# A decoder step on one core: layer 0's single-bank feed-forward stretch begins at part 1 instead of part 2

## Chip, cores and metric

One core of one Trainium2 chip. The metric is the device time of the whole program in microseconds. The kernel computes one inference step of a two-layer decoder for a prompt of 1024 tokens and eight sample tokens; nearly all of its work is matrix products on TensorE (PE).

## Reference

Layer 0 has a gated recurrence and attention to 256 memory tokens, layer 1 stick-breaking attention over a shared key and value store and again the memory attention. Behind each mixer stands a SwiGLU feed-forward network with 1024 model columns and 2816 inner ones. Cut to what the change touches:

```python
def swiglu(h, w_gu, w_down):
    gate, up = jnp.split(h @ w_gu, 2, axis=-1)
    return (jax.nn.silu(gate) * up) @ w_down

for l in range(DEPTH):                       # 2 layers
    hn = rmsnorm(h, g[0])
    mix = a_mixer(...) if l < N_A else b_mixer(...)
    h = h + rmsnorm(mix, g[1])
    h = h + rmsnorm(swiglu(rmsnorm(h, g[2]), w_gu[l], w_down[l]), g[3])
    if l == N_A - 1:                         # shared keys and values behind layer 0
        sb_k, sb_v = jnp.split(rmsnorm(h, g_kv) @ w_kv, 2, axis=-1)
```

## The kernel before

**Groups.** The tokens go in two groups: group 0 has 512 prompt tokens, group 1 the other 512 and the 8 sample tokens, 520 columns, worked on as two halves of 260. The groups run shifted against each other, so that the mixer of one lies beside the feed-forward network of the other: while group 0 is in the stick-breaking attention of layer 1 (`b0.sb`, 12 steps, and `b0.mem`, 8 steps), group 1 is in the feed-forward network of layer 0.

**Precision.** Each float32 operand is split into a rounded part (a cast on ScalarE, ACT) and a rest (a subtraction on VectorE, DVE). A product is three matmuls: high by high, high by low, low by high. Weights come in tiles of 4 x 128 rows by 128 columns (256 KB) by a DMA that SyncE (SP) issues, and are split when they have come; line 204 and 205 are that pair in `split_w`, 489 and 490 the same in `gate_up_w`.

**The feed-forward network.** Its 22 slices of 128 inner columns are made in five parts (`PARTS`: 5, 5, 4, 4 and 4 slices). A part makes its slices (gate, silu, up, product) and then adds its down projection, eight blocks in four steps, to the running sum R. So parts 0 and 1 have 9 steps each, the others 8. There are three ways to make a slice for group 1:

- in `ffn.part`, with `proj` (line 218): two projections of 48 matmuls with 260 columns. It uses a pool `mmp` of two double banks of the matmul accumulator (PSUM).
- in `ffn_w.part` with `gate_up_q` (line 453): the same 96 matmuls, in four single banks `Q(0)` to `Q(3)`. The first such slice puts its gate into two banks of the small pool that the attention also uses (`S`).
- in `ffn_w.part` with `gate_up_w` (line 499): gate and up, the two halves of the 1024 rows and the two halves of the columns are taken as a 2 x 2 block matrix product, which is made with 7 block products instead of 8: 7 x 12 = 84 matmuls. It needs sums of blocks of the weights and of the tokens.

The weight sums are made by `weight_sums` ahead of time and lie in device memory (`wsum`): for each part eight DMAs issued by GpSimd (POOL), four plain copies (line 556) and four that add (line 554). Each is paced by a mark, a small GpSimd copy (line 551) of the tile that `now[0]` names, and the transfer is issued behind it. For layer 0 they exist for parts 2, 3 and 4, for layer 1 for all parts.

The token sums are made by `sums_w` (lines 288 and 296 and the splits at 225 and 226), 16 steps, beside the first three slices of the single-bank stretch, which are made plainly by `gate_up_q` (`steps` (5, 6, 5) is the number of sum steps beside each). They take buffers of the pools `B` and `A`, which the attention uses too. `set_banks` closes one set of accumulator pools and opens the other.

**Order.** `weave` interleaves generators by the rates that are given with them; this sets the priorities. The framework then plans the instructions of each engine from these priorities and its own cost model: an instruction that is ready may pass one of higher priority that waits for a buffer or an operand. Buffers of a pool are handed out in turn. On the chip each engine then runs its fixed list.

Of the kernel before, what the change touches and what calls it, by code (L numbers as in the profile page):

```python
# [10 lines left out]
F32R = mybir.dt.float32r  # L11
# [7 lines left out]
P = 128  # L19
# [4 lines left out]
def tile_decoder(  # L24
# [25 lines left out]
    def nm(s):  # L50
        uid[0] += 1
        return f"{s}_{uid[0]}"
# [48 lines left out]
    def A(dt=F32):  # L101
        return apool.tile([P, 2, WID], dt, tag="a", name=nm("a"))
# [164 lines left out]
            out.append(x)  # L267
            yield

    def sums_w(xs, ops, YT):  # L270

        n, h = NG[1], PW[1]
        for k in range(4):
            x0, x1 = xs[k], xs[k + 4]
            y = YT()
            if k % 2 == 0:
                z, u = YT(), YT()
            o = (k % 2) * h  # L280
            ops.append([
                x0[:, :, :h], x1[:, :, :h], x1[:, :, h:n], z[:, :, o : o + h], u[:, :, o : o + h],
                y[:, :, :h], y[:, :, h : 2 * h],
            ])

            def full(x, c):
                t = B()
                nc.vector.tensor_add(t[:, :h], x[:, 0, c : c + h].bitcast(F32), x[:, 1, c : c + h].bitcast(F32))
                return t

            b11, b12, b21, b22 = full(x0, 0), full(x0, h), full(x1, 0), full(x1, h)
            for d, p, a, b in (
                (b11, u[:, :, o : o + h], b12, b11), (b12, y[:, :, h : 2 * h], b12, b22),
                (b22, y[:, :, :h], b22, b11), (b21, z[:, :, o : o + h], b21, b22),
            ):
                nc.vector.tensor_sub(d[:, :h], a[:, :h], b[:, :h])
                split_to((p[:, 0, :], p[:, 1, :]), d[:, :h])
                yield
# [15 lines left out]
    made = [None]  # L314

    def start(g, out):
        if g:
# [76 lines left out]
    class out_proj:  # L394


        def __init__(self, g, l, store, last=False):
            self.g, self.l, self.store, self.x, self.last = g, l, store, [], last
# [40 lines left out]
            yield  # L439
        htok.append((ht, hs_))  # L440

    def gate_up_q(l, f, xt, side, n_side, first):

        h, n = PW[1], NG[1]
        sg = T()
        for j in range(2):
            w = split_w(w_gu[l], 0, ND, j * DFF + f * P)
            pp = [Q(2 * j + a) if j or f != first else S() for a in range(2)]
            for k in range(ND):
                wh, wl = w[k]  # L450
                for wi, (wt, xi) in enumerate(((wh, 0), (wh, 1), (wl, 0))):
                    for a in range(2):
                        ins = nc.tensor.matmul(  # L453
                            pp[a][:, :h], wt, xt[k][:, xi, a * h : (a + 1) * h],
                            start=(k == 0 and wi == 0), stop=(k == ND - 1 and wi == 2),
                        )
# [12 lines left out]
        return mt  # L469

    def gate_up_w(l, f, ops, spl, raws):

        h, n = PW[1], NG[1]
        part, o = part_of(f)
        gate, up = f * P, DFF + f * P
        src = [
# [49 lines left out]
        now[0] = mt[:, 0, 0:1].bitcast(F32)  # L526
        return mt

    now = [None]
    act = [None]  # L530
    sums = {}

# [30 lines left out]
    class ffn_w:  # L563


        def __init__(self, l, x, steps, first, rows, R=None):
            self.g, self.l, self.x, self.ops, self.steps, self.rows = 1, l, x, [], steps, rows
            self.first, self.plain, self.n, self.r, self.pi = first, PARTS[first][0] + len(steps), 0, 0, 0
            self.R, self.acc = R, None
            self.half = []  # L570

            def YT():
                if rows:
                    return xpool.tile([P, 2, NG[1]], F32R, tag="x0", name=nm("y"))
                return A(F32R)

            self.sums = sums_w(x, self.ops, YT)

        def spl(self):
            self.n += 1  # L580
            if (self.pi or not self.rows) and self.n % 8 in (1, 4, 6):
# [18 lines left out]
            return wraw.tile([P, 4, P], F32, tag="w", name=nm("w"))  # L600

        def part(self, pi):
            l, n, h = self.l, NG[1], PW[1]
            f0, nf = PARTS[pi]
            last = pi == len(PARTS) - 1
            mids = []
            for j in range(nf):
                self.pi = pi
                if f0 + j < self.plain:
                    mids.append(gate_up_q(l, f0 + j, self.x, self.sums, self.steps[j], PARTS[self.first][0]))  # L610
                    now[0] = mids[-1][:, 0, 0:1].bitcast(F32)
                else:
                    mids.append(gate_up_w(l, f0 + j, self.ops, self.spl, self.raws))
                yield
            if pi == 0:
                self.R = R_one()
# [506 lines left out]
    def hgrn_prompt(g, Ft, Kt, Qt, Vt):  # L1123
# [15 lines left out]
        for lv in range(7):  # L1139
            m = 1 << lv  # L1140
            nbg = G // (2 * m)
            for hp in range(2):
# [8 lines left out]
                for hh in range(2):  # L1151
# [283 lines left out]
    with tc.issue_after(made[0].ins):  # L1435
# [73 lines left out]
    o0 = out_proj(0, 0, M)  # L1509
    drain(o0.mm(a0.xo))  # L1510
# [44 lines left out]
    drain(o1.mm(b1.xo))  # L1555
    weave((o1.finish(), 17), (f0.part(4), 8))
    set_banks(True)
    f1 = ffn_w(1, o1.x, (5, 6, 5), 0, True)
# [34 lines left out]
```

## Time and profile before

| | |
|---|---|
| median of 3 runs | 2496.46 us (2495.56 to 2497.24) |
| the profiled execution | 2497.11 us |
| its span | 2495.4 us |
| busy: PE, weight loads, DVE, ACT, GpSimd | 2461.4, 2155.8, 1598.1, 1196.8, 121.9 us |
| bytes moved | 391.26 MB, 157 GB/s over the span |
| matmuls of block products, L499, by operand | 1008, 912 and 432 |

The stages around the change, from the start of the span: the recurrent mixer of group 0 from about 84 to 196 us, the attention of group 0 beside parts 0 and 1 from about 1034 to 1229, parts 2 to 4 in single banks from 1253.75 to 1449. In the windows, a row gives a stretch, the busy time of each engine in it with the number of instructions, the granted clock (1.00 is full), the busy share of the 16 DMA engines and the bytes moved per second.

### The profile page before, as it was taken

The page shows a single profiled execution, that of the slowest core. Times are in us where ns is not written, and L with a number is a line of the kernel's source. Part 1 is how long each engine was busy: PE and PEld are TensorE (multiplying, and loading weights), DVE is VectorE, ACT ScalarE, POOL GpSimd, SP SyncE. Part 2 cuts the span into 40 slices and gives each one's busy share as a digit, 9 for nine tenths or more (in the row PEclk, how much of TensorE's full clock was granted, in tenths as well). Part 3 has the DMA queues.
Part 4 walks back from the last instruction along what each step waited for, and adds up shares of the span by engine and source line. Part 5 has one row for each costly group of instructions (what it writes and reads, how often), then busy time and mean ns, then how long its engine had stood idle before and what let it go on. Part 6 is the DMA issues. An engine that isn't in the chain of part 4 may idle for free.

```text
span 2495.4 us, 40868 instructions
## 1 busy us (share of the span) xinstructions
PE 2461.4 (99%) x15455; PEld 2155.8 (86%) x15455; DVE 1598.1 (64%) x2868; ACT 1196.8 (48%) x2289; POOL 121.9 (5%) x188
## 2 busy tenths in 40 slices
PE   8999999999999999999999999999999999999998
PEld 6888888877866898899999989977777798999998
DVE  5867556754765475665656575778677548855666
ACT  5437544243433454555544554555454345554445
POOL 1000000000010000000100100011000000000000
PEclk9999999999999999999999999999999999999999
DMA  5354666555786776566577746544343433464552
GB/s 190 111 165 119 162 184 157 132 141 150 223 204 184 197 185 194 165 156 167 134 199 193 226 140 187 160 145 144 102 140 119 122 120 114 141 186 144 148 148 73
DMA packets 521551, 391.26 MB, mean 157 GB/s; under 512 B 19973, under 2 KB 459858, under 8 KB 521354
## 3 DMA queue, kind: packets, MB, share of 16 engines
q1 hardware_dynamic: 493194, 308.94, 41.8%
q0 software_dynamic: 28160, 79.70, 13.5%
q8 instruction: 122, 2.00, 0.3%
q14 instruction: 75, 0.61, 0.1%
HBM read 358.76 MB, written 101.11 MB: 184 GB/s over the span
## 4 chain that ended last, share of the span: by engine, by line
PE 92%; DVE 4%; DMA 2%; ACT 1%; issue 1%; SPq 0%; DVEq 0%; ACTq 0%
PE mm L218 54%; PE q L499 11%; PE q L631 7%; PE s L1150 2%; PE mm L1018 2%; PE q L453 2%; PE s L1345 1%; PE s L1311 1%; PE s L885 1%; PE s L854 1%; PE mm L803 1%; PE mm L830 1%; PE q L663 1%; DMA c<-in_cache_mem_v 1%; PE ns L926 1%
## 5 line engine op out<-in xcount | busy, mean ns | idle before, releaser
L218 PE MATMUL mm<-x,ws 128*128 128x512 f32 (+1 forms) x6624 | 1215.0, 340 | 3.9 <-DVE r L390 1.5
L218 PEld LDWEIGHTS mm<-x,ws 128*128 128x128 f32 x6624 | 1012.5, 188 | 157.6 <-issue 14.6
L204 ACT CAST ws<-w 128x512 fp32r<-128x512 f32 (+1 forms) x672 | 395.3, 589 | 624.2 <-PE mm L218 477.8
L205 DVE TENSOR_TENSOR ws<-w,ws 128x512 fp32r<-128x512 f32 (+1 forms) x672 | 434.5, 650 | 270.5 <-ACT ws L204 263.8
L218 PE MATMUL mm<-m,ws 128*128 128x512 f32 (+1 forms) x1536 | 327.9, 366 | 4.7 <-DVE r L390 4.7
L218 PEld LDWEIGHTS mm<-m,ws 128*128 128x128 f32 x1536 | 253.2, 188 | 56.7 <-DVE r L390 7.3
L631 PE MATMUL q<-m,ws 128*128 128x260 f32 x1440 | 175.9, 283 | 0.0
L631 PEld LDWEIGHTS q<-m,ws 128*128 128x128 f32 x1440 | 173.4, 188 | 1.1 <-DVE t L522 0.5
L490 DVE TENSOR_TENSOR ws<-w,ws 128x512 fp32r<-128x512 f32 x164 | 112.4, 691 | 79.8 <-ACT ws L489 76.4
L489 ACT CAST ws<-w 128x512 fp32r<-128x512 f32 x164 | 101.4, 621 | 98.0 <-PE q L631 34.2
L499 PE MATMUL q<-x,ws 128*128 128x260 f32 x1008 | 134.3, 282 | 0.0
L499 PEld LDWEIGHTS q<-x,ws 128*128 128x128 f32 x1008 | 126.4, 188 | 0.0
L499 PE MATMUL q<-y,ws 128*128 128x260 f32 x912 | 119.3, 283 | 0.1
L499 PEld LDWEIGHTS q<-y,ws 128*128 128x128 f32 x912 | 113.5, 188 | 0.3 <-ACT q L506 0.3
L235 DVE TENSOR_SCALAR t<-mm 128x512 f32<-128x512 f32 (+1 forms) x70 | 48.3, 690 | 59.7 <-PE mm L218 59.4
L695 DVE TENSOR_TENSOR t<-t,mm 128x512 f32<-128x512 f32 (+1 forms) x54 | 37.2, 688 | 57.1 <-PE mm L218 57.1
L390 DVE TENSOR_TENSOR r<-r,mm 128x512 f32<-128x512 f32 (+1 forms) x72 | 49.3, 685 | 37.1 <-PE mm L218 36.2
L239 DVE TENSOR_TENSOR t<-t,t 128x512 f32<-128x512 f32 (+1 forms) x54 | 37.4, 692 | 55.1 <-ACT t L238 55.1
L226 DVE TENSOR_TENSOR m<-t,m 128x512 fp32r<-128x512 f32 (+1 forms) x88 | 60.9, 692 | 6.7 <-ACT m L225 5.3
L258 DVE TENSOR_TENSOR st<-st,n 128x512 f32<-128x512 f32 (+1 forms) x91 | 62.2, 691 | 3.0 <-ACT n L257 1.6
L225 ACT CAST m<-t 128x512 fp32r<-128x512 f32 (+1 forms) x88 | 54.9, 624 | 17.0 <-DVE t L695 7.7
L453 PE MATMUL q<-x,ws 128*128 128x260 f32 x480 | 61.0, 288 | 1.5 <-DVE ws L205 1.4
(344 smaller groups left out, 2850.5 us busy)
## 6 DMA issues: line engine op xcount, KB each, us to landing
w<-in_w_gu SPq DMA_DIRECT2D x310, 256.0 KB
w<-in_w_down SPq DMA_DIRECT2D x160, 256.0 KB
wsum<-in_w_gu POOLq DMA_DIRECT2D x36, 1024.0 KB, 9.4
w<-wsum SPq DMA_DIRECT2D x94, 256.0 KB
w<-in_w_in_a SPq DMA_DIRECT2D x80, 256.0 KB
w<-in_w_o SPq DMA_DIRECT2D x64, 256.0 KB
wsum<-in_w_gu POOLq DMA_DIRECT2D x12, 1280.0 KB, 11.4
wsum<-wsum POOLq DMA_DIRECT2D x12, 1024.0 KB, 5.6
```

The lines of the kernel that those rows point to most:

```text
L204: nc.scalar.copy(ws[:, 0, :n, :], raw[:, :n, :])
L205: nc.vector.tensor_sub(ws[:, 1, :n, :], raw[:, :n, :], ws[:, 0, :n, :].bitcast(F32))
L218: nc.tensor.matmul(ps[:, a, : PW[g]], wt, xt[k][:, xi, o : o + PW[g]], start=(k == 0 and wi == 0), stop=(k == nk - 1 and wi == 2),)
L225: nc.scalar.copy(dst[0], src)
L226: nc.vector.tensor_sub(dst[1], src, dst[0].bitcast(F32))
L258: nc.vector.tensor_add(acc[:, :n], acc[:, :n], t[:, :n])
L453: ins = nc.tensor.matmul(pp[a][:, :h], wt, xt[k][:, xi, a * h : (a + 1) * h], start=(k == 0 and wi == 0), stop=(k == ND - 1 and wi == 2),)
L489: nc.scalar.copy(w[:, 0, :], src)
L490: nc.vector.tensor_sub(w[:, 1, :], src, w[:, 0, :].bitcast(F32))
L499: nc.tensor.matmul(ps[:, :h], w[:, wj, k * P : (k + 1) * P], x[:, xi, :], start=(first and k == 0 and wi == 0), stop=(k == 3 and wi == 2), ...
L631: nc.tensor.matmul(pp[a][:, :h], wt, mids[k][:, xi, a * h : (a + 1) * h], start=(k == 0 and wi == 0), stop=(k == nf - 1 and wi == 2),)
L1018: nc.tensor.matmul(pb[i][:, a, :], xt[k][:, xi, c * P : (c + 1) * P], ws[:, s, :], start=(k == 0 and wi == 0), stop=(k == ND - 1 and wi == 2),
```

## The change

In layer 0, the two-bank form makes part 0 alone, and the single-bank stretch `ffn_w` makes parts 1 to 4. So slices 5, 6 and 7 (before: 10, 11 and 12) are the plain ones with the token sums beside them, and slices 8 to 21 (before: 13 to 21) go by the 7 block products. The weave of the attention holds 20 steps of attention, 9 of part 0 and 16 steps of layer 1's weight sums.

The weight sums of layer 0 are made for part 1 too, in the order 2, 3, 4, 1: 32 steps instead of 24. They begin one stage sooner, with eight steps woven into the recurrent mixer of group 0. So that the marks there follow the mixer, `now[0]` is set in `hgrn_prompt` to the decay tile behind its update. The other hunks pass the group as an argument and add an option `own`, which no call sets.

```diff
@@ hgrn_prompt
                 nb = 64 // m
+                now[0] = F_[:, 0, 0:1]
                 for hh in range(2):
@@ the order of the stages
     drain(a0.v(), a0.fq())
+    w0 = weight_sums(0, (2, 3, 4, 1))
     weave(
-        (a0.core(), 22),
+        (a0.core(), 22), (islice(w0, 8), 8),
         (chain(mem_load(), mem_keys(0), mem_values(0), mem_keys(1), mem_values(1), a0.qm(M)), 22),
     )
     a0.open()
     a1 = mixer_a(1, x1)
     weave((chain(a0.gate(), a0.merge()), 8), (start(1, x1), 14))
-    w0 = weight_sums(0, range(2, 5))
     weave((a0.mem(), 8), (a1.fq(), 8), (islice(w0, 6), 7))
...
     f1 = ffn(1, 0, o1.x)
-    weave((chain(b0.sb(), b0.mem()), 25), (chain(f1.part(0), f1.part(1)), 18), (islice(ws, 16), 17))
+    weave((chain(b0.sb(), b0.mem()), 20), (f1.part(0), 9), (islice(ws, 16), 17))
     set_banks(True)
-    fw = ffn_w(0, o1.x, (5, 6, 5), 2, False, f1.R)
-    weave((chain(fw.part(2), fw.part(3), fw.part(4)), 24), (islice(ws, 8), 8))
+    fw = ffn_w(1, 0, o1.x, (5, 6, 5), 1, False, f1.R)
+    weave((chain(fw.part(1), fw.part(2), fw.part(3), fw.part(4)), 33), (islice(ws, 8), 8))
```

More of the change, by code (lines that the diff above doesn't have):

```diff
@@ L268, in normed, with sums_w @@
             yield
-    def sums_w(xs, ops, YT):
-        n, h = NG[1], PW[1]
+    def sums_w(g, xs, ops, YT, ZT):
+        n = NG[g]
+        h = n // 2
         for k in range(4):
@@ L278, in sums_w @@
             if k % 2 == 0:
-                z, u = YT(), YT()
+                z, u = ZT(), ZT()
             o = (k % 2) * h
@@ L312, in rms_rows @@
         nc.vector.tensor_scalar(xt, xt, ss[:n], None, op0=ALU.mult)
-    made = [None]
+    made, now = [None], [None]
     def start(g, out):
@@ L440, in token_rows, with gate_up_q @@
         htok.append((ht, hs_))
-    def gate_up_q(l, f, xt, side, n_side, first):
-        h, n = PW[1], NG[1]
+    def gate_up_q(g, l, f, xt, side, n_side, first):
+        n = NG[g]
+        h = n // 2
         sg = T()
@@ L469, in gate_up_q, with gate_up_w @@
         return mt
-    def gate_up_w(l, f, ops, spl, raws):
-        h, n = PW[1], NG[1]
+    def gate_up_w(g, l, f, ops, spl, raws):
+        n = NG[g]
+        h = n // 2
         part, o = part_of(f)
@@ L527, in gate_up_w @@
         return mt
-    now = [None]
     act = [None]
@@ L563, in tile_decoder, with __init__ @@
     class ffn_w:
-        def __init__(self, l, x, steps, first, rows, R=None):
-            self.g, self.l, self.x, self.ops, self.steps, self.rows = 1, l, x, [], steps, rows
+        def __init__(self, g, l, x, steps, first, rows, R=None, own=False):
+            self.g, self.l, self.x, self.ops, self.steps, self.rows, self.own = g, l, x, [], steps, rows, own
             self.first, self.plain, self.n, self.r, self.pi = first, PARTS[first][0] + len(steps), 0, 0, 0
@@ L574, in YT @@
                     return xpool.tile([P, 2, NG[1]], F32R, tag="x0", name=nm("y"))
+                if own:
+                    return cpool.tile([P, 2, 512], F32R, tag="c", name=nm("y"))
                 return A(F32R)
-            self.sums = sums_w(x, self.ops, YT)
+            self.sums = sums_w(g, x, self.ops, YT, YT if rows else lambda: A(F32R))
         def spl(self):
             self.n += 1
-            if (self.pi or not self.rows) and self.n % 8 in (1, 4, 6):
+            if (self.pi or not self.rows) and not self.own and self.n % 8 in (1, 4, 6):
                 return cpool.tile([P, 2, 512], F32R, tag="c", name=nm("ws"))
@@ L602, in part @@
         def part(self, pi):
-            l, n, h = self.l, NG[1], PW[1]
+            g, l, n = self.g, self.l, NG[self.g]
+            h = n // 2
             f0, nf = PARTS[pi]
@@ L609, in part @@
                 if f0 + j < self.plain:
-                    mids.append(gate_up_q(l, f0 + j, self.x, self.sums, self.steps[j], PARTS[self.first][0]))
+                    mids.append(
+                        gate_up_q(g, l, f0 + j, self.x, self.sums, self.steps[j], PARTS[self.first][0])
+                    )
                     now[0] = mids[-1][:, 0, 0:1].bitcast(F32)
                 else:
-                    mids.append(gate_up_w(l, f0 + j, self.ops, self.spl, self.raws))
+                    mids.append(gate_up_w(g, l, f0 + j, self.ops, self.spl, self.raws))
                 yield
```

2 lines of the change are left out of this document (1 added, 1 removed).

## The prediction

> **What bounds the kernel now.** I read the page's head and its chain first, then the chain in order of time around the layer-0 feed-forward of group 1, then the windows and the groups of the stretches that the change touches.
>
> ```profile
> span 2495.4 us, 40868 instructions
> PE 2461.4 (99%) x15455; PEld 2155.8 (86%) x15455; DVE 1598.1 (64%) x2868; ACT 1196.8 (48%) x2289; POOL 121.9 (5%) x188
> PE 92%; DVE 4%; DMA 2%; ACT 1%; issue 1%; SPq 0%; DVEq 0%; ACTq 0%
> ```
>
> TensorE is busy 2461.4 of 2495.4 us and carries 92% of the chain. So time falls when matmuls go, provided that no new idle time opens; 34 us of idle time is all that is there today. The chain in order of time (start, length, what) gives the prices of the two ways to make a slice:
>
> ```profile
> 1253.75 5.73 PE s L453 x48
> 1259.47 28.70 PE q L453 x240
> 1288.17 10.10 PE q L499 x84
> 1321.74 40.37 PE q L499 x336
> 1517.89 5.75 PE mm L218 x48
> ```
>
> L453 is the plain slice in single banks (three slices: 288 matmuls in 5.73 + 28.70 us), L499 the slice by 7 block products (84 matmuls, 10.10 us; four of them 40.37), and L218 x48 is one projection of the two-bank form with 260 columns, 5.75 us, of which a slice needs two.
>
> The stretches (us, then busy time of PE, PEld, DVE, ACT, POOL, then clock, DMA share, GB/s):
>
> ```profile
> core 0: us, PE busy (x) PEld busy (x) DVE busy (x) ACT busy (x) POOL busy (x), PEclk, DMA share, GB/s
> 1034.00:1229.00 195.00, 194.34 (x1489) 183.85 (x1488) 109.11 (x201) 102.32 (x204) 15.28 (x28) 1.00 0.57 147
> 1226.00:1253.00 27.00, 27.00 (x222) 26.57 (x222) 25.35 (x65) 12.23 (x29) 4.54 (x4) 1.00 0.88 203
> 1253.75:1288.20 34.45, 34.45 (x290) 34.45 (x290) 17.35 (x32) 14.82 (x29) 1.24 (x2) 1.00 0.84 226
> 432.00:500.00 68.00, 68.00 (x407) 59.56 (x407) 48.79 (x135) 19.19 (x37) 5.88 (x12) 1.00 0.52 134
> 2113.00:2160.00 47.00, 44.54 (x341) 42.70 (x340) 45.55 (x98) 25.32 (x52) 0.00 (x0) 0.96 0.27 77
> 2130.00:2140.00 10.00, 9.27 (x64) 9.28 (x65) 8.86 (x22) 3.30 (x9) 0.00 (x0) 0.83 0.37 107
> 88.00:166.00 78.00, 78.00 (x577) 72.70 (x575) 65.71 (x168) 26.36 (x49) 0.00 (x0) 1.00 0.51 156
> 166.00:196.00 30.00, 30.00 (x164) 23.93 (x164) 11.37 (x23) 16.30 (x33) 0.00 (x0) 1.00 0.32 98
> 720.00:822.00 102.00, 94.65 (x400) 67.84 (x400) 65.34 (x112) 38.66 (x85) 8.36 (x12) 1.00 0.66 181
> 1253.00:1288.00 35.00, 35.00 (x295) 35.00 (x294) 17.48 (x31) 15.57 (x30) 1.24 (x2) 1.00 0.85 227
> ```
>
> **Removed: matmuls.** Of part 1's five slices, today each takes 2 x 5.75 = 11.50 us of PE. After the change the three plain slices of the single-bank stretch are 5, 6, 7 instead of 10, 11, 12 (same count, 34.43 us / 3 = 11.48 each), and slices 8 to 21 go by block products: five more slices at 10.09 (40.37 / 4) instead of 11.50. That is 5 x 1.41 = **7.0 us less PE**. The count agrees: 12 matmuls fewer per slice, 60 in all, at 40.37 / 336 = 0.120 us are 7.2. The down projections keep their number (part 1: 240 matmuls). PE is 100% busy in the neighbouring rows, so all of it lies on the path.
>
> **Added beside it, hidden.** A block-product slice splits 7 weight tiles, a plain one 4: 15 more casts and subtractions. In single-bank slices DVE and ACT have room (17.35 and 14.82 of 34.45 us above). Loads go from 4 to 7 tiles of 256 KB per slice, as in slices 13 to 21 today. The silu of part 1 becomes one table function; its load occurs once either way. I cost these at nothing; if the cover went, 15 x 0.69 = 10 us of DVE would stand in 50 us of PE, still no bound.
>
> **Moved: the attention of group 0 loses half its filler.** The 20 steps of b0.sb and b0.mem lie today beside two parts (18 steps), then beside one (9). Between 1034 and 1229 the two-bank matmuls are these, the rest is attention:
>
> ```profile
> L218 PE MATMUL mm<-x,ws 128*128 128x260 f32 (+1 forms) x966 | 127.1, 288 | 0.0
> L218 PE MATMUL mm<-m,ws 128*128 128x260 f32 x275 | 37.5, 289 | 0.0
> ```
>
> 1241 matmuls at 5.75 / 48 = 0.120 are 149 us, so attention is 194.3 - 149 = 45 us, 2.3 per step. Afterwards the stretch holds 45 us of it and part 0: 720 matmuls, 86 us; 131 us for 20 steps, 6.6 us a step where today it is 195 / 20 = 9.8. One step's own chain is shorter than that:
>
> ```profile
> 1077.95 0.26 DVE b L1324
> 1082.94 0.66 PE s L1340 x4
> 1222.50 0.86 PE s L854 x4
> 1227.69 1.10 PE s L885 x4
> ```
>
> 5.0 us from scores to the transposes in stick-breaking (1077.95 to 1082.94), 5.2 us from scores to values in memory attention, and the order keeps two stick-breaking units in flight. DVE's load: 109.1 less five slices of part 1 (each 4 splits and 4 other operations of about 0.69, 5.5 us) is 81 us in 131, 62%. The nearest row is 432 to 500, another 22-step mixer beside one nine-step part, with DVE at 72% and PE at 68.00 of 68.00. Bounds: from 0.66 us less (today's whole idle time there goes) to about 1 us on each of the 12 stick-breaking units. I take **+0.5**, by that nearest row.
>
> **Moved: the switch of banks, now right behind the attention.** Today attention ends 25 us before the switch; afterwards its last two steps stand behind the last step of part 0. Two things meet there. First, the gate of slice 5 takes its banks from the pool of the attention, so it waits for the last memory step; the up product and half of the next gate can run in between (48 + 24 matmuls, 8.6 us). Second, the 16 side sums for the block products take buffers that the attention uses: today they begin with its last step,
>
> ```profile
> 1226.82 0.76 DVE L288 TENSOR_TENSOR b<-x 128x260 f32<-128x260 f32 x2
> L296 DVE TENSOR_TENSOR b<-b,b 128x260 f32<-128x260 f32 x16 | 6.7, 420 | 0.0
> L226 DVE TENSOR_TENSOR a<-b,a 128x260 fp32r<-128x260 f32 x16 | 6.6, 421 | 0.5 <-ACT a L225 0.5
> L288 DVE TENSOR_TENSOR b<-x 128x260 f32<-128x260 f32 x16 | 6.3, 420 | 0.0
> L205 DVE TENSOR_TENSOR ws<-w,ws 128x512 fp32r<-128x512 f32 x17 | 11.6, 687 | 5.9 <-ACT ws L204 5.7
> ```
>
> and most of their 6.7 + 6.6 + 6.3 = 19.6 us lies under part 1's down projections. Afterwards all of it lies under slices 5 to 7: 12 splits (8.2) and about 9 smaller operations (4.6) make 32.4 us of DVE in 34.4 us of PE, and slice 8 needs the sums 1.4 us (12 matmuls) after its start. That is 94%, as in 1226 to 1253, where DVE was busy 25.35 of 27 and PE 27.00 of 27. Bounds: 0 by that row, 2.5 us of idle PE by 2113 to 2160, the same three slices in layer 1 with DVE at 97%. I take **+1.0**, nearer to the first, since our residual work there is smaller.
>
> The lower clock belongs to the upper bound: behind the gap in layer 1 the granted clock was 0.83 for 10 us, 1.7 us more. The Trainium skill (TensorE: Matmul & The Clock Gate, Part 1) says that the clock is halved after an idle window of about 3.4 us; by that rule gaps below it would cost only themselves, while here a shorter idle sum went with 0.83, and the trace decides.
>
> **Moved: eight weight-sum steps into group 0's recurrent mixer.** Layer 0's sums go from 24 to 32 steps, the first eight beside a0.core (88 to 196). Each is one GpSimd mark and one DMA:
>
> ```profile
> wsum<-in_w_gu POOLq DMA_DIRECT2D x36, 1024.0 KB, 9.4
> wsum<-wsum POOLq DMA_DIRECT2D x12, 1024.0 KB, 5.6
> ACT ws L204 <- PE mm L830: 11.8, 6, 2.6
> 119.68 1.73 PE s L1150 x16
> 121.41 2.85 PE mm L830 x12
> ```
>
> The new mark reads the decay tile, which VectorE rewrites two steps later; steps last 4.6 us (the last two rows, one of its steps and one of its neighbour's), sums come every 2.75 steps, 12.7 us, longer than a landing, so GpSimd's queue does not back up and the mark is read in time: nothing. The queue of SP isn't passed. The DMAs are 8.4 MB in 108 us that move 78 x 0.156 + 30 x 0.098 = 15.1 MB now: 23.5 MB, 218 GB/s. 1253 to 1288 carried 227 with PE full, and the casts here wait for PE (the third row, 11.8 us in six waits), not for loads. **0**; bounds under the second rival. The later places keep their counts of steps. In the attention 16 sums now come every 8 us instead of 12; GpSimd may wait for a landing, but nothing waits for a mark soon.
>
> **Sum.** -7.0 + 0.5 + 1.0 + 0 = -5.5 us. The profiled execution took 2497.11 us (span 2495.4 and 1.7 around it), 0.65 above the median 2496.46. So 2497.11 - 5.5 = 2491.6, and on the median's scale **2491.0 us**. A measurement of this kernel tells about 0.2%, 5.0 us, from no change.
>
> **Rival one: the switch eats more (gain of 1 to 5 us).** VectorE becomes the bound from the last attention step to slice 8, as in layer 1: 2.5 us idle and 1.7 us of clock instead of my 1.0, with 0.5 in the weave: -7.0 + 4.2 + 0.5 = -2.3, 2494.2 us. For it: the sums lose their cover and begin later than the FFN's own work. Against: 94% with PE full above. Chance 0.33.
>
> **Rival two, slower: DMA paces a0.core.** If the mixed traffic moves less than 218 GB/s, loads of memory weights come late and PE waits. At 181 GB/s, the rate of 720 to 822, where PE lost 7.35 us, 23.5 MB take 130 us instead of 108: +22, net +15 (2511). It passes no change below 23.5 MB / 115 us = 204 GB/s, and +5 below 196; at 190 it gives +16 - 5.5 = +10, 2507 us. For it: small stores of keys and values share the stretch. Against: 227 GB/s with PE full, tiles loaded well ahead. Chance 0.12. The Trainium skill (DMA: Bandwidth & Descriptors, SWDGE vs HWDGE vs iDMA) says each DMA engine takes turns between the queues of GpSimd's and SP's transfers; by that rule weight loads keep about half the rate while a sum is in flight, which speaks for this rival; that 227 was reached with both kinds running speaks for enough left.
>
> **Rival three: the attention's chain paces the weave.** If each stick-breaking unit waits another 1.5 us for DVE and ACT queues, 18 us: +11, 2507. Against it 432 to 500. Chance 0.05.
>
> **The numbers.** Forecast (gain of about 5 to 8 us) 0.50, rival one 0.33, two and three 0.17. Faster by over 0.2%: 0.48, within: 0.35, slower: 0.17. The range reaches from 2488.5 (7.2 by the count and 0.66 idle gone) through rival one and unchanged to 2500.0, leaving out most of rivals two and three.
>
> **What would show it.** L499 with 420 more matmuls, L218 with 480 + 240 fewer; L453 beginning about 86 us sooner against the attention's start; PE idle under 1.5 us from the attention's begin to slice 8; DVE over 90% in slices 5 to 7. Wrong if PE shows more than 3 us idle there, a clock under 1.00, or if ACT's casts between 88 and 196 wait for DMA.

## The result, and the profile after

The changed kernel takes **2509.55 us**, median of 5 runs (2506.26 to 2513.2), against 2496.22 (2494.68 to 2497.24) of the kernel before on the same chip: ratio 1.0054, 95% interval 1.004 to 1.0069. It is 13.3 us slower where 5.5 us less were forecast. The profiled execution took 2513.2 us, the longest of the five, so the stages below add up to more than 13.3 us.

The head of the profile after, and its row of GpSimd's queue:

```profile
span 2511.0 us, 40869 instructions
PE 2463.2 (98%) x15395; PEld 2153.2 (86%) x15395; DVE 1604.7 (64%) x2896; ACT 1202.6 (48%) x2314; POOL 136.9 (5%) x204
...
q0 software_dynamic: 31360, 90.18, 15.1%
```

There are 60 matmuls fewer, as counted, yet PE is busy 1.8 us longer and idle 13.8 us longer (47.8 against 34.0). The busy time grows because the granted clock was 0.5 for 27.3 us of the span instead of 10.2 (the last 4 us of each span left out), and matmuls take longer there: 96 of a down projection took 13.16 us from 1321.8 on, part of it at half clock, and 11.87 us from 1375.2 on at the full one. L502 is the block product, L499 before:

```profile
L502 PE MATMUL q<-x,ws x1188: 277/282/368, 1214.5 to 2473.2; 128*128 128x260 f32 x198
L502 PE MATMUL q<-a,ws x672: 277/283/387, 1217.3 to 1440.6; 128*128 128x260 f32 x168
```

With 912 unchanged that is 2772 against 2352: 420 more, 5 slices of 84, as forecast.

Where the time went is seen from the first matmul of each stage in the two traces (own differences of their start times, us): the recurrent mixer of group 0 up to that of group 1, from there to the stick-breaking attention of group 0, and from there to the last single-bank matmul of layer 0.

| stage | before | after | difference |
|---|---|---|---|
| mixer of group 0 | 309.5 | 316.5 | +7.0 |
| mixer of group 1 to attention | 642.4 | 646.2 | +3.8 |
| attention and feed-forward | 413.4 | 418.1 | +4.7 |
| all later stages together | 1046.8 | 1047.2 | +0.4 |

**The mixer.** The windows of after, and below them of before (us, busy time of PE, PEld, DVE, ACT, POOL, then clock, DMA share, GB/s):

```profile
84.00:196.00 112.00, 107.53 (x723) 96.59 (x722) 77.66 (x190) 39.18 (x72) 9.42 (x16) 0.97 0.76 207
100.00:120.00 20.00, 16.21 (x101) 14.86 (x100) 12.03 (x28) 4.26 (x8) 0.23 (x1) 0.83 0.77 196
```

```profile
84.00:196.00 112.00, 111.32 (x766) 99.79 (x765) 81.03 (x198) 45.28 (x88) 0.00 (x0) 1.00 0.45 138
100.00:120.00 20.00, 20.00 (x142) 18.47 (x141) 18.20 (x43) 6.41 (x12) 0.00 (x0) 1.00 0.59 174
```

All is lost between 100 and 120 us: 3.8 us of idle PE, and 6.8 us of half clock from 109.6 on, which make the clock of 0.83. What PE waited for there (engine, line, releaser: us, times, longest):

```profile
ACT t L815 <- DMA mks<-t: 5.0, 1, 5.0
...
PE mm L818 <- ACT t L815: 3.8, 1, 3.8
```

L815 copies new memory keys into a buffer of the pool `T`, which has three of them, and an earlier store from that buffer is still under way. The queues of SP and GpSimd (start, length of the issue; line 556 is the adding transfer in the changed kernel, 558 the plain one):

```profile
98.84 0.33 SPq L816 DMA_DIRECT2D mks<-t  x1
...
100.24 2.00 SPq L821 DMA_DIRECT2D out_mk_prompt<-t  x1
...
103.19 0.39 SPq L816 DMA_DIRECT2D mks<-t  x1
...
110.17 0.33 SPq L816 DMA_DIRECT2D mks<-t  x1
```

```profile
99.12 1.10 POOL L556 DMA_DIRECT2D wsum<-in_w_gu  x1
...
1307.62 1.04 POOL L556 DMA_DIRECT2D wsum<-in_w_gu  x1
...
1377.35 1.01 POOL L556 DMA_DIRECT2D wsum<-in_w_gu  x1
```

The copy of the fourth head's keys starts at 109.78. The row of waits above infers a store of keys (L816), but the landings, read from the semaphores of the trace, name another. The keys' store of 98.84 landed at 101.09, and that of 103.19 at 111.30, too late to have released the copy. The store of the transposed keys (L821), issued at 100.24, 1.1 us behind an adding sum transfer, landed at 109.62. Taken in turn, the three buffers give the fourth copy that store's buffer too. The next store of keys can be issued only at 110.17.

**The down projections.** The two other sums above stand 2 us behind the start of the down projections of parts 2 and 3 (L638). The chain in order of time there:

```profile
1265.25 40.41 PE q L502 x336
...
1307.06 3.00 DMA w<-in_w_gu
...
1311.46 8.60 DMA w<-wsum
1320.08 0.63 ACT ws L492
...
1321.34 0.43 DVE r L647
...
1321.81 13.16 PE q L638 x96
1334.97 40.38 PE q L502 x336
1375.35 3.10 PE q L638 x24
...
1379.89 6.82 DMA w<-wsum
```

The chain leaves PE: a load for the next part's first slice, issued at 1311.46, takes 8.60 us. ACT's cast (L492) waits for it, DVE's subtraction (L493) for the cast, and behind that in DVE's fixed list stands the addition of the finished block (L647), whose bank the down projection needs (the rows of waits for 1290 to 1420, then PE's for the whole stage):

```profile
ACT ws L492 <- DMA w<-wsum: 13.0, 3, 7.8
DVE ws L493 <- ACT ws L492: 31.4, 31, 7.4
```

```profile
PE q L638 <- DVE r L647: 5.9, 2, 4.5
PE q L502 <- DVE t L468: 1.3, 1, 1.3
```

```profile
1315.00:1320.00 5.00, 2.34 (x20) 2.13 (x18) 0.00 (x0) 0.00 (x0) 0.00 (x0) 1.00 1.09 275
1320.00:1335.00 15.00, 13.19 (x98) 13.15 (x99) 7.64 (x17) 3.52 (x6) 0.00 (x0) 0.89 0.33 95
```

In 1315 to 1320 ACT and DVE do nothing and PE stops at 1317.3, while the DMA engines are full; behind it the clock falls to 0.89. Before, the transfers issued within a down projection of the single-bank stretch were plain copies (line 556 of the kernel before), an add (554) 4.7 us before its end, and an add 12.7 us into the last one, which no further slice of the stretch follows:

```profile
1300.29 0.64 POOL L556 DMA_DIRECT2D wsum<-in_w_gu  x1
1317.02 1.07 POOL L554 DMA_DIRECT2D wsum<-in_w_gu  x1 [0.36 <-issue]
...
1369.55 0.66 POOL L556 DMA_DIRECT2D wsum<-wsum  x1 [0.32 <-issue]
...
1438.33 1.16 POOL L554 DMA_DIRECT2D wsum<-in_w_gu  x1 [0.33 <-issue]
```

After has a third such add, at 1443.20, 2.3 us into its last down projection, and PE does not wait within it. So the place alone does not decide; no slice of the stretch is loaded behind this one.

### The profile page after: what moved, and what is told of

Its sections match the earlier page's. It is cut to its first block, busy times and chain, and to the rows that moved or that the text cites. A ratio compares the mean times of both kernels' runs of the same rounds, so it can differ in the third digit from the quotient of the medians.

```text
span 2511.0 us, 40869 instructions
## 1 busy us (share of the span) xinstructions
PE 2463.2 (98%) x15395; PEld 2153.2 (86%) x15395; DVE 1604.7 (64%) x2896; ACT 1202.6 (48%) x2314; POOL 136.9 (5%) x204
## 3 DMA queue, kind: packets, MB, share of 16 engines
q0 software_dynamic: 31360, 90.18, 15.1%
## 4 chain that ended last, share of the span: by engine, by line
PE 47%; DVE 4%; DMA 2%; ACT 1%; issue 1%; DVEq 0%; ACTq 0%
PE mm L218 21%; PE q L502 13%; PE q L638 7%; PE q L670 1%; PE s L1353 1%; DMA w<-wsum 1%; PE s L1319 1%; PE ns L933 1%; PE s L1348 0%; PE s L892 0%; DVE ws L205 0%; PE s L861 0%; DVE b L297 0%; DVE b L1339 0%; DMA w<-in_w_gu 0%
## 5 line engine op out<-in xcount | busy, mean ns | idle before, releaser
L218 PE MATMUL mm<-x,ws 128*128 128x512 f32 (+1 forms) x6144 | 1153.4, 344 | 2.2 <-DVE t L235 1.3
L218 PEld LDWEIGHTS mm<-x,ws 128*128 128x128 f32 x6144 | 953.1, 188 | 155.9 <-issue 15.2
L218 PEld LDWEIGHTS mm<-m,ws 128*128 128x128 f32 x1296 | 227.0, 190 | 59.2 <-DVE r L391 9.0
L638 PE MATMUL q<-m,ws 128*128 128x260 f32 x1680 | 206.9, 284 | 5.9 <-DVE r L647 5.9
L638 PEld LDWEIGHTS q<-m,ws 128*128 128x128 f32 x1680 | 203.7, 189 | 7.5 <-DVE r L647 6.3
L493 DVE TENSOR_TENSOR ws<-w,ws 128x512 fp32r<-128x512 f32 x182 | 124.8, 690 | 94.7 <-ACT ws L492 90.1
L492 ACT CAST ws<-w 128x512 fp32r<-128x512 f32 x182 | 112.5, 621 | 109.1 <-PE q L638 34.5
L502 PE MATMUL q<-x,ws 128*128 128x260 f32 x1188 | 158.3, 282 | 0.0
L502 PEld LDWEIGHTS q<-x,ws 128*128 128x128 f32 x1188 | 149.0, 188 | 0.0
L502 PE MATMUL q<-y,ws 128*128 128x260 f32 x912 | 119.6, 283 | 0.2 <-ACT q L509 0.2
L502 PEld LDWEIGHTS q<-y,ws 128*128 128x128 f32 x912 | 113.6, 188 | 0.8 <-ACT q L509 0.4
L502 PE MATMUL q<-a,ws 128*128 128x260 f32 x672 | 88.0, 283 | 1.3 <-DVE t L468 1.3
L502 PEld LDWEIGHTS q<-a,ws 128*128 128x128 f32 x672 | 83.8, 188 | 1.5 <-DVE t L468 1.5
L391 DVE TENSOR_TENSOR r<-r,mm 128x512 f32<-128x512 f32 x64 | 43.8, 684 | 37.0 <-PE mm L218 36.2
L647 DVE TENSOR_TENSOR r<-r,q 128x260 f32<-128x260 f32 x112 | 42.5, 421 | 37.0 <-PE q L638 36.8
```

The source lines that it names most:

```text
L218: nc.tensor.matmul(ps[:, a, : PW[g]], wt, xt[k][:, xi, o : o + PW[g]], start=(k == 0 and wi == 0), stop=(k == nk - 1 and wi == 2),)
L391: nc.vector.tensor_add(dst, dst, pv(ps, g))
L492: nc.scalar.copy(w[:, 0, :], src)
L493: nc.vector.tensor_sub(w[:, 1, :], src, w[:, 0, :].bitcast(F32))
L502: nc.tensor.matmul(ps[:, :h], w[:, wj, k * P : (k + 1) * P], x[:, xi, :], start=(first and k == 0 and wi == 0), stop=(k == 3 and wi == 2), ...
L638: nc.tensor.matmul(pp[a][:, :h], wt, mids[k][:, xi, a * h : (a + 1) * h], start=(k == 0 and wi == 0), stop=(k == nf - 1 and wi == 2),)
```

## The experiments

**Theory:** the saved matmuls are worth what was forecast, and transfers of weight sums that now meet small stores and loads of SP cost more. **Rivals:** the shorter weave of the attention or the switch of banks costs by itself; or the loss in the mixer is the amount of DMA work, not one late store. Each run was compared with runs of the kernel before on its chip (medians 2493.78 to 2495.15), so rows are to be compared by their ratios. Stages as in the table above, from the profiled execution of each; "layer 1" is its stretch from the attention of group 1 to the single banks:

| kernel | median us | ratio to before | mixer | to attention | feed-forward | layer 1 |
|---|---|---|---|---|---|---|
| before | | 1 | 309.5 | 642.4 | 413.4 | 522.1 |
| after | 2509.55 | 1.0054 [1.004, 1.0069] | 316.5 | 646.2 | 418.1 | 523.4 |
| e1 | 2506.31 | 1.005 [1.0035, 1.0066] | 313.2 | 641.5 | 416.7 | 522.9 |
| e2 | 2520.94 | 1.0093 [1.0077, 1.011] | 315.9 | 645.6 | 408.5 | 546.8 |
| e3 | 2518.25 | 1.0093 [1.0076, 1.011] | 314.1 | 644.3 | 408.6 | 541.7 |
| e4 | 2500.35 | 1.0027 [1.0017, 1.0037] | 316.7 | 638.8 | 413.1 | 522.5 |
| e5 | 2501.44 | 1.003 [1.0017, 1.0043] | 314.9 | 636.8 | 414.6 | 523.5 |
| e6 | 2507.89 | 1.006 [1.0043, 1.0077] | 314.5 | 641.0 | 414.2 | 523.9 |
| e7 | 2506.16 | 1.0051 [1.0035, 1.0068] | 309.6 | 642.6 | 418.4 | 523.6 |
| e8 | 2492.09 | 0.999 [0.9981, 1.0] | 309.5 | 631.7 | 411.3 | 526.7 |
| e9 | 2498.51 | 1.0019 [1.001, 1.0028] | 312.7 | 632.7 | 416.5 | 526.5 |
| e10 | 2495.13 | 0.9999 [0.999, 1.0008] | 310.8 | 643.1 | 416.5 | 522.5 |
| e11 | 2497.86 | 1.0014 [1.0001, 1.0028] | 311.6 | 635.5 | 417.2 | 523.6 |
| e12 | 2491.84 | 0.9986 [0.9977, 0.9995] | 309.5 | 640.3 | 408.4 | 523.4 |
| e13 | 2494.41 | 0.9996 [0.9987, 1.0005] | 309.6 | 640.2 | 413.2 | 522.0 |
| e14 | 2488.28 | 0.9972 [0.996, 0.9984] | 309.5 | 632.7 | 409.2 | 526.7 |
| e15 | 2486.84 | 0.9975 [0.9965, 0.9985] | 309.6 | 634.1 | 413.1 | 522.5 |
| e16 | 2501.06 | 1.0031 [1.0019, 1.0043] | 318.0 | 631.5 | 418.1 | 523.0 |

**e1: the first eight sums behind the mixer.**

```diff
-        (a0.core(), 22), (islice(w0, 8), 8),
+        (a0.core(), 22),
-    weave((chain(a0.gate(), a0.merge()), 8), (start(1, x1), 14))
+    weave((chain(a0.gate(), a0.merge()), 8), (start(1, x1), 14), (islice(w0, 8), 8))
```

> The changed kernel, but the first eight weight-sum steps of layer 0 stand beside the gate of group 0 (166 to 232 us in the kernel before, 81 to 98 GB/s moved there) instead of beside its recurrent mixer. Theory 1 (a sum transfer of 1 MB holds up the stores and loads issued behind it for about 10 us, and this costs wherever the instruction behind has no slack): the 3.8 us idle time of PE before the transposes of the memory keys and the 6.8 us of half clock behind it go, so 6 to 8 us less than the changed kernel, about 2502.5. Theory 2 (the loss lies in the attention with half its filler and in the side sums of slices 5 to 7): no change, about 2509.5.

A miss on the size: the gap at 106 us is gone, but a gap of 2.10 us opens at 232 us, with 3.4 us of half clock behind it (its waits: engine, line, releaser):

```profile
DVE a L1248 <- POOL mk L553: 3.2, 1, 3.2
...
PE mm L218 <- DVE x L350: 2.1, 1, 2.1
```

DVE cannot overwrite a tile before GpSimd's late mark has read it. Half of the stage's 7 us is back; the ratio shows little of it (1.005 against 1.0054).

**e2: the eight sums out of the single-bank stretch**, into the attention of group 1.

```diff
-    weave((chain(fw.part(1), fw.part(2), fw.part(3), fw.part(4)), 33), (islice(ws, 8), 8))
+    drain(fw.part(1), fw.part(2), fw.part(3), fw.part(4))
...
-        (chain(f0.part(0), f0.part(1), f0.part(2), f0.part(3)), 34),
+        (chain(f0.part(0), f0.part(1), f0.part(2), f0.part(3)), 34), (ws, 10),
```

> The changed kernel, but the last eight weight-sum steps of layer 1 leave the single-bank stretch of layer 0 and stand beside the attention of layer 1 (1600 to 1950 in the kernel before, 104 to 158 GB/s). Theory 1: the 4.5 and 1.4 us idle times at the start of two down projections and 1.7 us of clock go, 6 to 8 us less than the changed kernel, about 2502.5. Theory 2: within 1.5 us of the changed kernel.

The feed-forward stage falls to 408.5, 4.9 below the kernel before; the cost is only moved, and grows: layer 1's attention is 23 us longer, PE waiting there for ACT and DVE (the longest of its waits):

```profile
PE s L1353 <- ACT b L1350: 9.1, 3, 4.2
```

**e3: both moves at once** (the edits of e1 and e2).

> Both moves together. Theory 1: 13 to 15 us less than the changed kernel, about 2495 to 2496, so level with the kernel before or up to 2 us faster; the saved 7 us of matmuls then still pay for 1 to 2 us at the switch and for jitter of the recurrent stage of group 1. Theory 2: over 2505.

A miss on the time, as in e2. The two stages add up (314.1 and 408.6), and layer 1 pays again: moving the sums settles the place of the loss, not a cure.

**e4: the kernel before, with its sums begun early.** No matmul is changed.

```diff
+                now[0] = F_[:, 0, 0:1]
...
+    w0 = weight_sums(0, range(2, 5))
     weave(
-        (a0.core(), 22),
+        (a0.core(), 22), (islice(w0, 8), 8),
```

> The kernel before with one part of the change alone: layer 0's 24 weight-sum steps begin beside the recurrent mixer of group 0, eight of them there, paced by its decay tile; parts 1 to 4 are made as before. Theory 1: the mixer stage loses 6 to 8 us, about 2503. Theory 2, and any theory by which the place of the sums costs nothing: 2496, within 1.5 us.

The early sums alone cost 6 us in the median, by the same wait in the kernel before (its keys are copied at L807):

```profile
ACT t L807 <- DMA mks<-t: 5.1, 1, 5.1
```

**e5: sum transfers in rows of 512 bytes** (the adds in two halves of the rows).

```diff
-                        nc.gpsimd.dma_start(d, a, accum_op=ALU.add)
+                        for r in (0, 256):
+                            nc.gpsimd.dma_start(
+                                d[r : r + 256], a[r : r + 256], accum_op=ALU.add, max_dma_last_dim=512)
...
-                        nc.gpsimd.dma_start(d, a, max_dma_last_dim=4 * w)
+                        nc.gpsimd.dma_start(d, a, max_dma_last_dim=512)
```

> The changed kernel with the same weight-sum bytes at the same places, but in rows of 512 bytes instead of 2048 or 2560 (each adding transfer in two halves). Theory 1, made sharper by the packets of the trace (while an adding transfer runs, its packets of 2048 bytes and the loads' packets of 512 bytes start in about equal number, 80 per us each, so loads fall from about 320 to 41 KB per us): with equal packets loads keep about 90 KB per us, the idle times of 3.8, 4.5 and 1.4 us shrink to about a third, 5 to 9 us less than the changed kernel, about 2502. Theory 3 (loads behind a sum wait for the whole sum, by bytes, whatever the packets): no change or slower, since the sums take longer.

8 us faster than the changed kernel in the median, 6 by the ratios: the gap of 3.79 us becomes 2.04, that of 4.47 becomes 1.66. But of the profiled execution's gain only 1.6 and 3.5 us stand in these two stages, and 9.4 in the stage between them, so the gain is not shown to come from the two gaps. Its row of the queue, with a third more time for the same bytes:

```profile
q0 software_dynamic: 94144, 90.19, 20.0%
```

**e6: the eight sums of the single-bank stretch tied to steps**, so that none is issued into the start of a down projection.

```diff
-    weave((chain(fw.part(1), fw.part(2), fw.part(3), fw.part(4)), 33), (islice(ws, 8), 8))
+    for i, _ in enumerate(chain(fw.part(1), fw.part(2), fw.part(3), fw.part(4)), 1):
+        if i in (1, 2, 4, 10, 11, 18, 19, 26):
+            next(ws)
```

> The changed kernel, but the eight weight-sum steps in the single-bank stretch are put behind named steps, the four adding ones behind a slice that is followed by another slice, none behind the last slice of a part. Theory 1: what costs is that an adding transfer starts with the down projection, whose matmuls are few per weight tile and behind which the next part's tiles are loaded; the idle times of 4.5 and 1.4 us go, the stretch from the attention's start to the last single-bank matmul takes 409 to 411 us instead of 418, total 7 to 9 us less than the changed kernel, about 2502. A theory by which any sum in that stretch costs 4 us: no change.

A miss on the size (414.2 where 409 to 411 was expected, and no gain in the ratio). The two waits at the down projections are gone, and one of 3.91 us stands at slice 8, again behind a late load:

```profile
ACT ws L492 <- DMA b<-wsum: 7.0, 1, 7.0
...
PE q L502 <- DVE t L468: 3.9, 1, 3.9
```

**e7: the key copies get buffers of another pool;** every transfer keeps its place in the order.

```diff
-            src = T()
+            src = N()
```

> The changed kernel with the memory keys copied out of the accumulator into a buffer of another pool (two buffers of its own), so that the copy shares no buffers with the token rows; the sums stay beside the mixer. Theory 1: the 3.8 us idle time there is a wait for a buffer whose store is late; with buffers of its own the first stores have two heads more time, the idle time falls below 1.5 us and the half clock behind it goes, 4 to 7 us less, about 2504. If the loads of memory weights were late as well (rival two of the prediction as it was told), the idle time only moves: within 1.5 us of 2509.5.

```profile
84.00:196.00 112.00, 111.32 (x768) 99.82 (x766) 81.16 (x198) 45.27 (x88) 9.86 (x16) 1.00 0.79 213
```

The mixer stage is 309.6, that of before, with more bytes per second than in after. So in this stage neither amount nor rate was the loss, but the wait for a buffer of `T`. What that is worth in the whole time is not shown: the median is 3.4 us below after's, by the ratios it is under 1 us, and the four executions lie at 2503.8, 2504.13, 2508.2 and 2508.52, of which the first was traced.

**e8: sums only for the slices that use them,** in new places. The plain slices need no sums: part 1's then have 256 columns instead of 640, and layer 1's part 0's too. `SKIP` shortens them; e1's move and e6's places are added, and part 1's sums come first.

```diff
+    SKIP = {(0, 1): 3, (1, 0): 3}
...
+            s = SKIP.get((l, i), 0)
+            f0, nf = f0 + s, nf - s
...
-    w0 = weight_sums(0, (2, 3, 4, 1))
+    w0 = weight_sums(0, (1, 2, 3, 4))
```

> A version that should beat both kernels: the single-bank stretch begins at part 1 as in the change; weight sums are made only for slices that use them (2 of 5 in part 1 of layer 0 and in part 0 of layer 1, 8 + 8 transfers of 0.5 instead of 1.25 MB), part 1's eight come first and beside the gate of group 0, the rest of layer 0's stand where the kernel before has them, and the eight of layer 1 stand as in the run before this one. Theory 1: the matmuls' 7 us with about 2 us given back, 2489 to 2492, 4 to 6 us under the kernel before. Theory 2 of the first four runs (attention and side sums): 2500 or more.

The first changed version that isn't slower than before. Two gaps are left: 2.72 us at 1193.8, slice 8 again, and 2.30 at 1708.7. Its stage before the attention is 10.7 us shorter than before's, which the change does not explain.

**e9: e8 with e5's rows; e10: the kernel before with e5's rows; e11: e5 and e7 together.**

> The trimmed and moved version with the sum transfers cut into 512-byte rows. Theory one (each 2048-byte sum packet that stands between two 512-byte packets of SyncE's queue delays loads and stores, wherever a sum runs): small packets cost less delay, and the small gaps that the trimmed version still has (2.72 us at 1193.8, 2.30 at 1708.7) shrink: 2488 to 2490 us, ratio 0.997 to 0.998 to the kernel before. Rival (the trimmed version has already no transfer left that meets a wait): 2492 as without it, within 1 us.

> The kernel before, with nothing but its sum transfers cut into 512-byte rows: a control for the run of the changed kernel with small packets. Theory one (packet sizes cost time wherever a sum runs beside a step that needs loads, so also before the change): 2488 to 2491 us, the stage from group 1's mixer to the stick-breaking attention about 637 us instead of 642.4. Rival (only the places that the change added are hurt): 2494 to 2495, no difference.

> The changed kernel, its order untouched, with both mendings at once: key copies in their own pool, sum transfers in 512-byte rows. If the two costs are separate, the mixer stage is 309.6 us as with the pool alone, the stage behind it 637 and the feed-forward stage 414.6 as with small packets alone: 2501.4 less 5.3 is 2496 us. If the small packets had already taken away what the pool takes away, 2501, no better than small packets alone.

Theory one misses in e9 and e10. In the kernel before small rows gain nothing (e10). e9 is 6.4 us slower than e8 in the median: its gap at slice 8 is 1.74 us instead of 2.72, but 3.4 us of half clock now follow it, and gaps of 1.76 us at 231.5 and 1.28 at 1300.8 are new. The medians of e5 and e11 differ by 3.6 us, with overlapping spreads and on different chips, and e11's stages of 311.6 and 417.2 miss the 309.6 and 414.6 that were expected. So it is not shown that the two costs are separate.

**e12: the changed kernel without the two sets of sums;** the slices concerned read plain blocks of the weights in their place, and the sums of parts 2 to 4 begin behind the mixer, as in the kernel before. e13 is the same for the kernel before, which has only the second set.

```diff
+            if (l, i) in ((0, 1), (1, 4)):
+                sums[l][i] = (a11, a12, a21, a22)
+                continue
```

> The changed kernel, with the two sets of eight sum steps that stand in the wrong places left out: those of layer 0's part 1 and those of layer 1's part 4 (their slices read blocks of the weights themselves in place of the sums, by the same loads, so those products are not the reference's). The remaining sums stand where they stand in the kernel before. Theory (the excess comes from these transfers alone, and the matmuls saved are worth what the forecast took): mixer stage 309.5 us, feed-forward stage 408.5, the rest as before, 2489 to 2490.5 us, ratio 0.998. Rival (the shorter weave of the attention, the switch of banks and the smaller room for splits cost something by themselves): feed-forward stage 413 or more, 2494 or slower.

> The kernel before without the eight sum steps of layer 1's part 4, which stand beside its single-bank stretch too (those slices read blocks of the weights in place of the sums). A control: if the transfers cost nothing there, since they do not meet the start of a down projection, 2494.5 us within 1.5, feed-forward stage 413; if any sum beside the single-bank stretch costs, 2490 or less, and then part of what the run without sums gains is not the matmuls'.

PE's waits of e12 over the whole attention and feed-forward stage (the two longest):

```profile
PE s L1351 <- ACT b L1345: 0.6, 2, 0.3
PE s L1322 <- DVE b L1335: 0.6, 1, 0.6
```

Nothing waits at the switch of banks, at slice 8 or at a down projection. The stage is 4.8 us shorter than e13's, and the mixer is as before. Against after (ratio 0.9986 against 1.0054) the time falls by 17 us: the whole loss goes with these two sets of sums (7.0 and 9.7 by the stages). The medians of e12 and e13 differ by 2.6 us, less than the stage, as layer 1 took 1.4 us longer in e12's profiled execution and the stretch behind it as much again, where e12 has 3.4 us of half clock at 2125.9 and e13 none.

**e14: e8 with the first copies behind slices 8 and 9.**

```diff
-        if i in (1, 2, 4, 10, 11, 18, 19, 26):
+        if i in (4, 5, 10, 11, 12, 18, 19, 26):
```

> The trimmed and moved version with the first two of the eight steps, plain copies, behind slices 8 and 9 instead of 5 and 6 (and the third and fourth behind the first slices of part 2). Theory (the copies at 1181 and 1185 us delay the first block load of slice 8: a gap of 2.72 us): the gap is below 1 us, the feed-forward stage 408.5 to 410 instead of 411.3, and 2489.5 us instead of 2492. Rival (any place has its own late load): another gap of 2 us or more opens, and 2492 to 2496.

The gap before slice 8 is gone, no wait of PE in the stage is over 0.6 us, and the version beats the kernel before and the changed one.

**e15: the kernel before with the trim alone** (`SKIP = {(1, 0): 3}`); **e16: the changed kernel with the trim alone.**

> The kernel before with one thing from the best version: layer 1's first sums made for the two slices that use them (256 columns instead of 640), no other edit. If the trim alone took away the gap of 5 us near 720 us: the stage from group 1's mixer to the stick-breaking attention 633 us instead of 642, 2487 to 2490 us, ratio 0.996 to 0.998, and the best version's lead over the kernel before is then this trim, with only 0 to 3 us left for the change itself. If the stage keeps 640 to 642 and the time 2494 to 2495, the lead is the change's.

> The changed kernel with the trim alone (sums only for the slices that use them, in both layers), every transfer in the place that the change gives it. Theory (place and size both count): the mixer stage stays near 314 to 316 us, since its first sums are of full width, the feed-forward stage at 418, and the stage between falls to 633 to 636 us: 2498 to 2502 us, ratio 1.002 to 1.003. Rival (the volume was the whole trouble): 2490.

Windows of the kernel before, then of e15:

```profile
640.00:720.00 80.00, 80.00 (x350) 64.31 (x348) 51.28 (x74) 31.25 (x54) 7.34 (x10) 1.00 0.86 240
720.00:830.00 110.00, 102.65 (x435) 74.28 (x435) 69.07 (x118) 41.41 (x90) 8.36 (x12) 1.00 0.67 182
```

```profile
640.00:720.00 80.00, 79.55 (x347) 63.54 (x345) 54.29 (x76) 30.21 (x54) 7.35 (x10) 1.00 0.70 197
720.00:830.00 110.00, 107.91 (x459) 79.17 (x460) 68.78 (x119) 44.58 (x94) 10.04 (x14) 1.00 0.59 161
```

With 0.70 of the DMA engines instead of 0.86 in use, PE is busy 5 us longer in the second stretch. e15 leads the kernel before by as much as e14 does: the lead of e14 is the trim, not the change. In e16 the mixer and the feed-forward stage are as slow as in after. The trim leaves the transfers in these two places at their full size, so e16 says that the loss there does not hang on the volume elsewhere, and that the trim alone brings after some 6 us by the ratios.

## Why the prediction was wrong

- **Removed, -7.0: held within a microsecond.** 60 matmuls went. In the attention and feed-forward stage, where neither has half clock, PE is busy 6.2 us less in e12 than in e13.
- **Attention with half its filler (+0.5) and switch of banks (+1.0): held within a microsecond.** e12's stage less e13's is -4.8 where -5.5 was forecast, and PE is idle in it for 2.05 us instead of 0.67, 1.4 more where 1.5 was forecast. From the attention's start to slice 8, e12 has one gap of over 0.5 us, 0.58. The reason for the +1.0 was off: DVE was to be over 90% busy in slices 5 to 7, and in after it is 32.46 of 41 us, with PE at 40.86. The amount of work was told rightly (32.4); the stretch is longer than the 34.4 us of its own matmuls, as the last memory-attention steps run in it:

```profile
1047.00:1175.00 128.00, 126.13 (x941) 116.73 (x940) 75.52 (x145) 71.50 (x149) 17.65 (x32) 1.00 0.78 195
1175.00:1216.00 41.00, 40.86 (x324) 39.61 (x322) 32.46 (x80) 23.19 (x54) 9.08 (x2) 1.00 0.61 163
```

  Rival one falls with it: the 1.27 us at slice 8 in after end with a load of 6.88 us, issued at 1207.76 behind the last of DVE's token sums, while a weight sum issued at 1203.49 was in flight. e12 has the same token sums and no weight sum there, and no gap.
- **"Moved: eight weight-sum steps into group 0's recurrent mixer: 0": the step that failed first.** It cost 7.0 us. The argument compared bytes per second over 108 us and looked at casts that wait for loads; it did not look at small stores that hold a buffer, nor at what a single transfer does to SP's queue for some 9 us. That GpSimd's transfers do not pass through SP's queue did not help, since the packets of the two queues slow each other (last section). The row of 227 GB/s on which the 0 rested holds one sum, a plain copy issued at 1267.33, and no add. Rival two named the place and the small stores, but as a matter of a rate below 204 GB/s, and e7 ran at 213 with PE full. Its sign, casts that wait for loads, did come: 4.5 us between 80 and 200 in after, none before; but e7 has 4.6 us of such waits and loses nothing, so they were not the cause. (Rival two's bounds take the gain as 7.0 us in most places and as 5.5 in one; with 5.5 throughout, 181 GB/s gives +16, and the bounds are 207 and 198 GB/s.) The Trainium skill (DMA: Bandwidth & Descriptors, SWDGE vs HWDGE vs iDMA) has the engines take turns between the queues; the prediction's "half the rate" is not what that means here, see below.
- **"The later places keep their counts of steps": the second, and dearer.** The counts were kept, but a stretch with 33 steps instead of 24 set the same eight sums against other work: two adds came 2 us into a down projection. The stage is 418.1 with them, 408.4 without (e12), 9.7 us, of which the gaps of 4.47, 1.40 and 1.27 us and 3.4 us of half clock explain 8.8; in the kernel before the eight cost 0.2 (413.4 and 413.2 in e13). The prediction had no rival for it; its sign of being wrong, PE idle for more than 3 us, was written for the time up to slice 8 (2.0 us in after, 3.3 with the gap at slice 8), and the gap of 4.47 us stands 100 us behind that.
- **The sum.** 7.0 in the mixer, 9.7 - 4.8 - 0.2 = 4.7 in the feed-forward stage, 3.8 between them and about 0.1 in all the rest: 15.6 us of span. The 3.8 stay open: e6 and e7 have the same sums there and took 641.0 and 642.6, so it is probably one execution's own, where a gap of 4.68 us was followed by 6.8 us of half clock; e13, without the change, has the like (4.86 and 6.8). Nothing was tried on it. Layer 1's stretch, which the forecast left alone, is 522.9 to 523.9 us in after, e1, e5 to e7, e11, e12 and e16, against 522.0 to 522.5 in before, e4, e10, e13 and e15: about 1 us, of open cause. Nor is it settled why e8, e9 and e14 have a gap at 1709 to 1719 us, which eats what the change gains in e14; in e14 DVE waits 3.9 us before it for a gathered load of cached values, against 0.8 in e15.

## What to carry to other kernels

A transfer that is moved must be laid against what the other queue does in the 9 to 10 us behind its issue, stores that hold buffers and loads whose consumers stand ahead of others in a fixed list, not against an average rate. When a loop gets longer, look where each step beside it now falls, even if their number stays. And give a new version's gain to the kernel before as well: here the trim of unneeded sums, found on the way, was worth as much without it, 0.25% (0.15 to 0.35%).

## What the runs showed of the hardware

Packets of the two queues in after, counted from its trace by the microsecond in which they start (GpSimd's sums beside SP's loads and stores):

```
us      sums: packets, KB    SP: packets, KB
1305         0     0.0          441   217.7
1312        77   157.7           58    29.7
1313        79   161.8           79    40.4
1314        84   172.0           81    41.5
1317         9    12.3          645   319.6
```

While a sum runs, both queues move about as many packets, but a sum's has 2048 bytes and a load's 512: SP is left with 41 KB in a microsecond, an eighth of the 320 that it moved alone. The Trainium skill (DMA: Bandwidth & Descriptors, SWDGE vs HWDGE vs iDMA) says that an engine changes queues only at packet boundaries; the trace agrees so far as the packets of the two queues come in about equal number, and shows that the shares then go by packet size. Yet making the sums' packets small was no cure (e9, e10): in e5 they took 20.0% of the engines' time instead of 15.1.

The half clock comes in pieces. In after, the granted clock is 0.5 for 6.8 us from 109.6 (gap 3.79 us), 6.8 from 730.9 (4.68) and 3.4 from 1321.4 (4.47); in e1 a gap of 2.10 us was followed by 3.4 us of it, in e8 one of 2.72 at 1193.8 by none. The Trainium skill (TensorE: Matmul & The Clock Gate, Part 1) tells of a free-running window of about 3.4 us; multiples of 3.4 agree, and so does that a gap's length alone does not decide.
